# Attention beside dense products: remainders on GpSimd, rows of ones kept, a norm square with priority

## The chip, the cores and the metric

The kernel runs on one core of a Trainium2 chip. A core has a matrix engine (TensorE, PE in the profile), a vector engine (VectorE, DVE), a scalar engine (ScalarE, ACT), GpSimd (POOL) and SyncE (SP, which issues most transfers). Each engine runs its own instructions strictly in order, and they wait for one another by semaphores. SBUF is the working memory of 128 partitions, PSUM holds the eight banks that TensorE writes. The metric is device time in microseconds (us), as a median over runs.

## The reference

The program is a decoder trunk of two layers on 512 tokens of width 1024, in float32. Each layer adds half a SwiGLU feed-forward network (FFN), then a mixer, then half of another FFN:

```
x = x + 0.5 * swiglu(rms_norm(x), ffn1_w_in, ffn1_w_out)
h = rms_norm(x) @ w_mix_in
y = concat[ short_conv(c_x, c_b, c_c), hgrn2(q, f, i, g), fox(q, k, v, f) ]
x = x + y @ w_mix_out
x = x + 0.5 * swiglu(rms_norm(x), ffn2_w_in, ffn2_w_out)
```

Only the mixer is touched by the change. Its three parts are:

- a gated causal convolution of width 3 over 256 channels;
- HGRN2, a linear recurrence with 4 heads of 64, whose output o of each head is normalised, o * rsqrt(mean(o * o) + eps), then scaled and gated;
- FoX attention with 8 heads of 64: logits q.k + c_t - c_s with c the running sum of log forget gates, a causal softmax, and the product with the values.

## The kernel before

**Exact products.** TensorE multiplies in a rounded format (fp32r), so each operand is split in two: a rounded part hi and the remainder lo = x - hi. A product is three matmuls (`mm3`, lines 322, 330 and 331): hi by hi, hi by the other's lo, lo by the other's hi. For weights the split is made while they stream: `granule` (line 286) loads two blocks of rows into one of two staging buffers `st` (line 294, on SyncE's queue), and `parted` (line 303) rounds them by ScalarE (line 311) and subtracts on VectorE (line 312) into one of three buffers `hl`. Both are issued under `high_priority`, so that they run ahead of the products that use them. A staging buffer is loaded again when its subtraction is done; an `hl` buffer is written again when its products are done.

**The mixer.** `mix` first projects features, then runs HGRN2 with the projections of attention's q, k and v (`fox_qkv`) beside it, and then attention with the remaining dense products beside it. `fox_attend` is a generator over 16 items (4 heads of one half, 4 blocks of 128 queries each); `beside` draws one dense granule per item. The first half of the heads has `conv` beside it: the features of the convolution, three streams of four granules, 256 columns wide. The second half has `most` beside it: four column groups of the output projection, over five of its eight row blocks, so three granules each (the third is of one row block, half as wide). After both, the last three row blocks of the output projection follow by themselves.

**Attention.** For each head, `fox_prep` makes four operands QA, QB, KA and KB: two transposed halves of q and k with their remainders, and in rows 64 and 65 of KB the negated running sums of log forget gates (a transfer, line 1556), against rows 64 and 65 of QB, which hold ones (a memset on GpSimd, line 1557). Two more transfers, lines 1565 and 1566, copy across partitions. Scores are two matmuls (lines 1586 and 1587) into a bank with the tag "sc"; VectorE subtracts the row maximum from it (line 1591), ScalarE exponentiates, and P is scaled by the reciprocal of its sum (lines 1595 to 1599). Then TensorE transposes P into a bank with the tag "pt" (line 1651), ScalarE rounds (1653) and VectorE subtracts (1654), and the products with the values follow (1609). PSUM has three banks "mm", two "sc", two "pt" and one "po".

**The norm of HGRN2.** At the end of `hgrn`, TensorE puts the means of o * o into two banks "pt" (line 1463). Then come ln and exp on ScalarE for a first inverse root r, the square of r (line 1471, an `act`, which the profile shows as line 274), and on VectorE, for each of the two halves, (mean + eps) * r * r (line 1473), which is the last reading of a bank. Lines 1476 to 1485 finish and split the result. These run while the first items of attention go by.

**What sets the order.** A planner places the instructions of each engine before the run: it takes the work in program order as its rank, `high_priority` raises the rank of what is issued under it, and of the instructions that are ready in its own reckoning the best rank goes first. On the chip the order is then fixed.

Of the kernel before, what the change touches and what calls it, by code (L numbers as in the profile page):

```python
# [8 lines left out]
F32 = mybir.dt.float32  # L9
F32R = mybir.dt.float32r  # L10
# [13 lines left out]
P = 128  # L24
# [133 lines left out]
class Trunk:  # L158
# [124 lines left out]
        self.chain[engine] = i.ins.name  # L283


    def granule(self, parts, kk, ahead=True, skew=0, keep=False, queued=False, first=False):
        nc = self.nc
        c = sum(ap.shape[1] for ap in parts)
        st = self.wp.tile([P, 1024], F32, tag="st", name=self.n("st"), bufs=2)
        s3 = st[:, : kk * c].rearrange("p (k c) -> p k c", k=kk)  # L290
        at = 0
        for ap in parts:
            w = ap.shape[1]
            d = nc.sync.dma_start(s3[:, :, at : at + w], ap.rearrange("(k p) c -> p k c", p=P))
            if queued:
                self.follow("s", d)
            at += w
        with self.tc.high_priority() if ahead and not keep else ExitStack():
            hi, lo = self.parted(st[:, : kk * c], 1 if ahead else kk, skew, keep or first)
        h3, l3 = (a.rearrange("p (k c) -> p k c", k=kk) for a in (hi, lo))  # L300
        return [(h3[:, i, :], l3[:, i, :]) for i in range(kk)]

    def parted(self, src, pieces=1, skew=0, keep=False):
        nc = self.nc
        n = src.shape[1]
        hl = self.wp.tile([P, 2 * 1024 + 64], F32R, tag="hl", name=self.n("hl"), bufs=3)
        hh, ll = (hl[:, a + skew : a + skew + n] for a in (0, 1024))
        w = n // pieces
        for c in range(0, n, w):
            hi, lo = hh[:, c : c + w], ll[:, c : c + w]  # L310
            a = nc.scalar.copy(hi, src[:, c : c + w])  # L311
            b = nc.vector.tensor_sub(lo, src[:, c : c + w], hi)  # L312
            if pieces > 1 or keep:
                self.follow("a", a)
                self.follow("v", b)
        return hh, ll
# [19 lines left out]
        for _ in self.stream_steps(*args, **kw):  # L336
            pass

    def stream_steps(self, jobs, parts_of, act, nk, mid=None, pre=None, given=None, queued=False, ending=None):
        k = 0  # L340
        while k < nk:
            kk = min(2, nk - k)
            if callable(mid) and k == nk - 2:
                mid()
            if pre is not None:
                pre(k)
            end = k + kk == nk
            if end and ending is not None:
                jobs = ending
            skew = SKEW_MOVING if jobs[0][2] is not None and jobs[-1][0].shape[-1] < T else 0  # L350
            keep = given is not None and given(k)
            rows = self.granule(
                parts_of(k, kk), kk, pre is None, skew, keep, queued, queued and k == 0
            )
            if keep:
                yield
            order = (
                [(job, j) for job in jobs for j in range(kk)]
                if end
                else [(job, j) for j in range(kk) for job in jobs]  # L360
            )
            for n, ((acc, cols, toks, *more), j) in enumerate(order):
                if pre is not None and n == len(order) // 2:
                    pre(k, True)
                if isinstance(mid, tuple) and (k, len(order) // 2) == (mid[0], n):
                    mid[1]()
                ah, al = act(k + j)
                hi, lo = rows[j]
                first, last = k + j == 0 and not more, end and j == kk - 1
                if toks is None:  # L370
                    self.mm3(acc, hi[:, cols], lo[:, cols], ah, al, first, last)
                else:
                    self.mm3(acc, ah[:, toks], al[:, toks], hi[:, cols], lo[:, cols], first, last)
            k += kk
            yield
# [647 lines left out]
    def mix(self, l, w, w_out, conv_w, out_gain, q_gain, k_gain, f_bias, next_gain):  # L1023
# [3 lines left out]
        with tc.tile_pool(name=self.n("mix"), bufs=1) as mp:  # L1027
# [23 lines left out]
            def cols(*spans):  # L1051
                return lambda k, kk: [w[k * P : (k + kk) * P, a : a + n] for a, n in spans]

            def features_steps(spans, banks, mid=None):
                bs = [self.bank(t) for t in banks]
                yield from self.stream_steps(
                    [(b, c, None) for b, c in zip(bs, FM2)], cols(*spans), self.xact, KD, mid
                )
                return bs

# [77 lines left out]
            for part, n in enumerate(hgrn):  # L1138
                if n is None:
                    break  # L1140
                if n == 0:
                    left.close()
                    ap1 = left.enter_context(
                        tc.tile_pool(name=self.n("at"), bufs=1, reuse_waits="tile")
                    )
                    for tag in ("PH", "PL"):
                        ap1.tile([P, 4, 2, P], F32R, tag=tag, name=self.n(tag), bufs=2)
                    ops = {h: self.fox_prep(ap1, h, half[0][0], qkg, "sc") for h in range(2)}
                if part < 2:
                    next(decay, None)  # L1150
                for _ in range(n):
                    next(dense, None)
# [18 lines left out]
            def conv():  # L1171
                for i in range(2):
                    bx, bc = yield from features_steps(
                        [(C_X + i * P, P), (C_C + i * P, P)], ("mm", "mm")
                    )
                    if i == 0:
                        inv2 = ap2.tile([P, T], F32, tag="t", name=self.n("iv2"), bufs=self.tb)
                        nc.scalar.activation(inv2, inv, AF.Square)
                    self.conv_in(ap2, i, bx, bc, inv2, cw)
                bb = yield from features_steps([(C_B, 256)], ("mm", "mm"))  # L1180
                for i in range(2):
                    self.conv_out(ap2, i, bb[i])

# [19 lines left out]
            def act(k0):  # L1203
                return lambda k: (self.yh[order[k0 + k]], self.yl[order[k0 + k]])
# [4 lines left out]
            def most():  # L1209
                for dg in range(4):  # L1210
                    banks = [self.bank("mm") for _ in range(2)]
                    yield from self.stream_steps(
                        [(bk, c, None) for bk, c in zip(banks, FM2)],
                        rows(0, 256 * dg, 256), act(0), 5,
                    )
                    for i in range(2):
                        add(2 * dg + i, banks[i])
# [47 lines left out]
    def hgrn(self, l, hp, hb, z, q, v, sg, og):  # L1265
# [202 lines left out]
        for x in range(2):  # L1468
            self.act(span(r, x), mb[x], AF.Ln, bias=self.epsc)
        self.act(r, r, AF.Exp, scale=-0.5)  # L1470
        self.act(t, r, AF.Square)
        for x in range(2):
            nc.vector.scalar_tensor_tensor(
                out=span(t, x), in0=mb[x], scalar=EPS, in1=span(t, x), op0=ALU.add, op1=ALU.mult
            )
        nc.vector.tensor_scalar(t, t, scalar1=-0.5, scalar2=1.5, op0=ALU.mult, op1=ALU.add)
        nc.vector.tensor_mul(r, r, t)
        nc.vector.tensor_mul(o, o, r)
# [73 lines left out]
    def fox_prep(self, pool, h, qk, g, tag="pt"):  # L1552
        nc = self.nc
        tl = lambda p, tag: pool.tile([p, T], F32R, tag=tag, name=self.n(tag), bufs=2)
        QA, QB, KA, KB = tl(P, "QA"), tl(66, "QB"), tl(P, "KA"), tl(66, "KB")
        nc.sync.dma_start(KB[64:66, :].bitcast(F32), self.negc[h : h + 1, :, :].bitcast(F32))
        nc.gpsimd.memset(QB[64:66, :].bitcast(F32), 1.0)
        b = self.bank(tag)
        for i in range(4):
            nc.tensor.transpose(  # L1560
                b[:, i * P : (i + 1) * P], qk[:, i, h % 4].rearrange("p w d -> p (w d)"), self.ident
            )
        nc.scalar.activation(QA[:64, :], b[:64, :], AF.Copy, scale=g[:64, :])
        nc.scalar.activation(KA[64:, :], b[64:, :], AF.Copy, scale=g[64:, :])
        nc.sync.dma_start(QB[:64, :].bitcast(F32), QA[:64, :].bitcast(F32))
        nc.sync.dma_start(KA[:64, :].bitcast(F32), KA[64:, :].bitcast(F32))
        nc.vector.scalar_tensor_tensor(
            out=QA[64:, :], in0=b[:64, :], scalar=g[:64, :], in1=QA[:64, :],
            op0=ALU.mult, op1=ALU.subtract,
        )  # L1570
        nc.vector.scalar_tensor_tensor(
            out=KB[:64, :], in0=b[64:, :], scalar=g[64:, :], in1=KA[64:, :],
            op0=ALU.mult, op1=ALU.subtract,
        )
        return QA, QB, KA, KB
# [297 lines left out]
```

## Time and profile before

| what | value |
|---|---|
| median of 3 runs | 1807.59 us (1806.88 to 1808.02) |
| the profiled execution, its own time | 1808.44 us |
| its span, first to last instruction | 1806.7 us |
| granted TensorE clock | 1.00 |
| TensorE busy | 1795.8 us (99%) |
| VectorE busy | 1453.4 us (80%) |
| ScalarE busy | 1000.7 us (55%) |
| GpSimd busy | 170.4 us (9%) |
| HBM read | 223.98 MB |

The profile is one execution. A row of instructions names the line, the engine, the operation, what is written and read, the shape, the count, the busy time and the mean duration in ns, and then how long the engine stood idle before them and which work ended that idle time. A row of waits names who waited for whom, the sum in us, how often, and the longest. Matmuls are pipelined: the next begins before the last has ended, so the time between two starts tells more than a duration.

### The profile page before, as it was taken

What the parts mean: (1) busy time and instruction counts of PE and PEld (TensorE: products, weight loads), DVE (VectorE), ACT (ScalarE), POOL (GpSimd) and SP (SyncE); (2) the same over time, 40 slices, a digit from 0 to 9 for tenths busy, and PEclk for the clock granted to TensorE, in tenths of its full rate; (3) what the DMA queues carried; (4) which work ended last, traced back from release to release, by engine and by line L of the source; (5) the groups of instructions that cost most, each with busy time, mean ns of one, the idle gap of its engine ahead of it and who ended that gap; (6) DMA issues with size and microseconds to landing.
All of it is one profiled execution on the core that took longest, in us unless ns stands there. A gap on an engine that the chain in (4) does not pass through costs nothing.

```text
span 1806.7 us, 34748 instructions
## 1 busy us (share of the span) xinstructions
PE 1795.8 (99%) x14267; PEld 1681.3 (93%) x14267; DVE 1453.4 (80%) x2036; ACT 1000.7 (55%) x1437; POOL 170.4 (9%) x172
## 2 busy tenths in 40 slices
PE   9999999999999999999999999999999999999999
PEld 7899999899888899999889999998998888999997
DVE  8889787776887898879679887876868878888893
ACT  5455554464786465556446555555547855555551
POOL 0011120100000001112001111201000000020210
PEclk9999999999999999999999999999999999999999
DMA  7668783233323767868265787823333247687762
GB/s 203 182 142 186 178 178 98 72 79 83 88 74 111 218 140 161 198 160 169 82 205 133 165 189 191 169 66 81 78 89 89 71 138 188 164 159 192 159 134 94
DMA packets 243486, 250.94 MB, mean 139 GB/s; under 512 B 18520, under 2 KB 228192, under 8 KB 243328
## 3 DMA queue, kind: packets, MB, share of 16 engines
q1 hardware_dynamic: 189424, 182.38, 33.8%
q0 software_dynamic: 53600, 66.09, 23.2%
q8 instruction: 112, 1.84, 0.4%
q14 instruction: 46, 0.38, 0.1%
q10 hardware_dynamic: 304, 0.27, 0.0%
HBM read 223.98 MB, written 2.10 MB: 125 GB/s over the span
## 4 chain that ended last, share of the span: by engine, by line
PE 92%; DVE 3%; ACT 3%; issue 1%; DMA 1%; SPq 0%; ACTq 0%; DVEq 0%
PE mm L322 13%; PE mm L330 13%; PE mm L331 13%; PE sc L330 6%; PE sc L331 6%; PE sc L322 6%; PE pt L322 6%; PE pt L330 6%; PE pt L331 6%; PE po L330 4%; PE po L322 4%; PE po L331 4%; ACT hl L311 1%; PE po L1609 1%; PE pt L1651 1%
## 5 line engine op out<-in xcount | busy, mean ns | idle before, releaser
L803 ACT CAST hl<-w 128x1024 fp32r<-128x1024 f32 x322 | 336.7, 1050 | 313.7 <-PE mm L331 82.4
L805 DVE TENSOR_TENSOR hl<-w,hl 128x1024 fp32r<-128x1024 f32 x322 | 392.2, 1221 | 80.7 <-ACT hl L803 80.7
L312 DVE TENSOR_TENSOR hl<-st,hl 128x512 fp32r<-128x512 f32 (+3 forms) x192 | 162.3, 845 | 106.3 <-ACT hl L311 105.5
L311 ACT CAST hl<-st 128x512 fp32r<-128x512 f32 (+3 forms) x192 | 142.6, 743 | 169.9 <-PE po L331 64.6
L322 PE MATMUL mm<-xc,hl 128*128 128x256 f32 (+1 forms) x733 | 201.2, 276 | 0.0
L330 PE MATMUL mm<-xc,hl 128*128 128x256 f32 x728 | 201.2, 276 | 0.0
L331 PE MATMUL mm<-xc,hl 128*128 128x256 f32 x728 | 201.0, 276 | 0.0
L322 PE MATMUL sc<-xc,hl 128*128 128x256 f32 (+1 forms) x532 | 146.0, 276 | 0.0
L330 PE MATMUL sc<-xc,hl 128*128 128x256 f32 x528 | 146.0, 276 | 0.0
L331 PE MATMUL sc<-xc,hl 128*128 128x256 f32 x528 | 145.9, 276 | 0.0
L322 PEld LDWEIGHTS mm<-xc,hl 128*128 128x128 f32 x733 | 137.4, 188 | 0.2
L330 PEld LDWEIGHTS mm<-xc,hl 128*128 128x128 f32 x728 | 136.7, 188 | 0.0
L331 PEld LDWEIGHTS mm<-xc,hl 128*128 128x128 f32 x728 | 136.7, 188 | 0.0
L322 PE MATMUL pt<-xc,hl 128*128 128x256 f32 (+1 forms) x482 | 132.6, 276 | 0.0
L330 PE MATMUL pt<-xc,hl 128*128 128x256 f32 x480 | 132.6, 276 | 0.0
L331 PE MATMUL pt<-xc,hl 128*128 128x256 f32 x480 | 132.5, 276 | 0.0
L322 PE MATMUL mm<-x,hl 128*128 128x512 f32 x272 | 107.4, 395 | 0.0
L331 PE MATMUL mm<-x,hl 128*128 128x512 f32 x272 | 106.4, 391 | 0.0
L330 PE MATMUL mm<-x,hl 128*128 128x512 f32 x272 | 106.1, 390 | 0.0
L322 PEld LDWEIGHTS sc<-xc,hl 128*128 128x128 f32 x532 | 99.7, 188 | 0.2
L331 PEld LDWEIGHTS sc<-xc,hl 128*128 128x128 f32 x528 | 99.1, 188 | 0.1
L330 PEld LDWEIGHTS sc<-xc,hl 128*128 128x128 f32 x528 | 99.2, 188 | 0.0
(513 smaller groups left out, 5594.1 us busy)
## 6 DMA issues: line engine op xcount, KB each, us to landing
w<-in_ffn_w_in_dram SPq DMA_DIRECT2D x140, 512.0 KB
w<-in_ffn_w_out_dram SPq DMA_DIRECT2D x64, 512.0 KB
w<-in_ffn_w_out_dram POOLq DMA_DIRECT2D x56, 512.0 KB, 8.3
st<-in_w_mix_in_dram SPq DMA_DIRECT2D x88, 256.0 KB
st<-in_ffn_w_in_dram SPq DMA_DIRECT2D x70, 256.0 KB
w<-in_ffn_w_in_dram POOLq DMA_DIRECT2D x35, 512.0 KB, 8.5
w<-S POOLq DMA_DIRECT2D x35, 512.0 KB, 4.7
st<-in_ffn_w_out_dram SPq DMA_DIRECT2D x24, 512.0 KB
```

The lines of the kernel that those rows point to most:

```text
L311: a = nc.scalar.copy(hi, src[:, c : c + w])
L312: b = nc.vector.tensor_sub(lo, src[:, c : c + w], hi)
L322: i = nc.tensor.matmul(acc[:, c], ah, bh[:, c], start=first and c.start == 0, stop=False, skip_group_check=True,)
L330: nc.tensor.matmul(acc, a, b, start=False, stop=False, skip_group_check=True)
L331: i = nc.tensor.matmul(acc, c, d, start=False, stop=last, skip_group_check=True)
L803: A(nc.scalar.copy(hi, src))
L805: return lambda: V(nc.vector.tensor_sub(lo, src, hi))
L1609: nc.tensor.matmul(self.ob[:, t0 + u * P : t0 + 2 * P], V[:, j, h % 4].rearrange("p a d -> p (a d)"), part[:, j, u:, :].rearrange("p i t - ...
L1651: nc.tensor.transpose(tb[:, j * P : (j + 1) * P], p[:, j * P : (j + 1) * P], self.ident)
```

## The change

It has four parts, all in the mixer, and so each occurs once per layer.

1. `granule`, `parted`, `stream_steps` and `features_steps` take an argument `lows`, the engine that subtracts. `conv` and `most` pass GpSimd; every other stream keeps VectorE. So 12 granules of `conv` and 12 of `most` have their remainders from GpSimd, in each layer. Their rounding stays on ScalarE, and their priority stays.
2. The tiles QB are no longer allocated for each head. Two are made once per layer, in the pool of attention, and used in turn.
3. Their rows of ones are written there, two memsets in each layer in place of eight.
4. In `hgrn`, the square of r and the two operations of line 1473 are issued under `high_priority`.

```
     def granule(self, parts, kk, ..., first=False, lows=None):
...
-            hi, lo = self.parted(st[:, : kk * c], 1 if ahead else kk, skew, keep or first)
+            hi, lo = self.parted(
+                st[:, : kk * c], 1 if ahead else kk, skew, keep or first, lows or nc.vector
+            )
...
-    def parted(self, src, pieces=1, skew=0, keep=False):
+    def parted(self, src, pieces=1, skew=0, keep=False, lows=None):
...
             a = nc.scalar.copy(hi, src[:, c : c + w])
-            b = nc.vector.tensor_sub(lo, src[:, c : c + w], hi)
+            b = (lows or nc.vector).tensor_tensor(lo, src[:, c : c + w], hi, op=ALU.subtract)
...
                         ap1.tile([P, 4, 2, P], F32R, tag=tag, name=self.n(tag), bufs=2)
+                    self.qb = pair(ap1, "QB", F32R)
+                    for t in self.qb:
+                        nc.gpsimd.memset(t[64:66, :].bitcast(F32), 1.0)
                     ops = {h: self.fox_prep(ap1, h, half[0][0], qkg, "sc") for h in range(2)}
...
                     bx, bc = yield from features_steps(
-                        [(C_X + i * P, P), (C_C + i * P, P)], ("mm", "mm")
+                        [(C_X + i * P, P), (C_C + i * P, P)], ("mm", "mm"), lows=nc.gpsimd
                     )
...
-                bb = yield from features_steps([(C_B, 256)], ("mm", "mm"))
+                bb = yield from features_steps([(C_B, 256)], ("mm", "mm"), lows=nc.gpsimd)
...
-                        rows(0, 256 * dg, 256), act(0), 5,
+                        rows(0, 256 * dg, 256), act(0), 5, lows=nc.gpsimd,
...
-        self.act(t, r, AF.Square)
-        for x in range(2):
-            nc.vector.scalar_tensor_tensor(
-                out=span(t, x), in0=mb[x], scalar=EPS, in1=span(t, x), op0=ALU.add, op1=ALU.mult
-            )
+        with self.tc.high_priority():
+            self.act(t, r, AF.Square)
+            for x in range(2):
+                nc.vector.scalar_tensor_tensor(
+                    out=span(t, x), in0=mb[x], scalar=EPS, in1=span(t, x),
+                    op0=ALU.add, op1=ALU.mult,
+                )
...
-        QA, QB, KA, KB = tl(P, "QA"), tl(66, "QB"), tl(P, "KA"), tl(66, "KB")
+        QA, KA, KB = tl(P, "QA"), tl(P, "KA"), tl(66, "KB")
+        QB = self.qb[h % 2][:66, :]
         nc.sync.dma_start(KB[64:66, :].bitcast(F32), self.negc[h : h + 1, :, :].bitcast(F32))
-        nc.gpsimd.memset(QB[64:66, :].bitcast(F32), 1.0)
```

More of the change, by code (lines that the diff above doesn't have):

```diff
@@ L283, in follow, with granule @@
         self.chain[engine] = i.ins.name
-    def granule(self, parts, kk, ahead=True, skew=0, keep=False, queued=False, first=False):
+    def granule(self, parts, kk, ahead=True, skew=0, keep=False, queued=False, first=False, lows=None):
         nc = self.nc
@@ L337, in stream, with stream_steps @@
             pass
-    def stream_steps(self, jobs, parts_of, act, nk, mid=None, pre=None, given=None, queued=False, ending=None):
+    def stream_steps(self, jobs, parts_of, act, nk, mid=None, pre=None, given=None, queued=False, ending=None, lows=None):
         k = 0
@@ L352, in stream_steps @@
             rows = self.granule(
-                parts_of(k, kk), kk, pre is None, skew, keep, queued, queued and k == 0
+                parts_of(k, kk), kk, pre is None, skew, keep, queued, queued and k == 0, lows
             )
@@ L1052, in cols, with features_steps @@
                 return lambda k, kk: [w[k * P : (k + kk) * P, a : a + n] for a, n in spans]
-            def features_steps(spans, banks, mid=None):
+            def features_steps(spans, banks, mid=None, lows=None):
                 bs = [self.bank(t) for t in banks]
                 yield from self.stream_steps(
-                    [(b, c, None) for b, c in zip(bs, FM2)], cols(*spans), self.xact, KD, mid
+                    [(b, c, None) for b, c in zip(bs, FM2)], cols(*spans), self.xact, KD, mid,
+                    lows=lows,
                 )
```

## The prediction

> **What bounds the kernel now.** I read the page's engine shares, then TensorE's own waits, then busy time by stretches of the two attention stages, then the order of time where TensorE stands longest, and last what GpSimd does there.
>
> ```profile
> span 1806.7 us, 34748 instructions
> PE 1795.8 (99%) x14267; PEld 1681.3 (93%) x14267; DVE 1453.4 (80%) x2036; ACT 1000.7 (55%) x1437; POOL 170.4 (9%) x172
> ```
>
> TensorE is busy for 1795.8 of 1806.7 us; all that other engines can give back is the 10.9 us in which it stands, and a little that its pipelined ends hide. What it waits for:
>
> ```profile
> PE pt L1651 <- DVE T L1473: 2.6, 2, 1.5
> PE mm L1765 <- DVE z L1752: 1.2, 1, 1.2
> PE po L1609 <- ACT PH L1653: 0.8, 2, 0.4
> PE sc L1586 <- DVE nm L1591: 0.7, 2, 0.4
> PE pt L1651 <- DVE KB L1571: 0.4, 2, 0.2
> PE mm L322 <- DVE zf L1125: 0.4, 1, 0.4
> PE sc L1586 <- DVE fo L1623: 0.2, 1, 0.2
> PE po L1609 <- DVE PL L1654: 0.2, 1, 0.2
> ```
>
> Line 1765 is the opening of the kernel and line 1125 lies ahead of attention. All else, 4.9 us, lies in the two attention stages, one per layer. The reader should see that the largest, 2.6 us, is two waits, one per layer, of a transpose for the HGRN2 norm, and that VectorE ends nearly all the others. Here are the two stages, and the first layer's worst 20 us (columns: stretch, its length, busy time and instructions of TensorE, its weight loads, VectorE, ScalarE, GpSimd, then the granted clock, DMA share and GB/s):
>
> ```profile
> 460.00:568.00 108.00, 105.15 (x585) 87.79 (x585) 90.09 (x222) 82.11 (x186) 3.13 (x6) 1.00 0.33 90
> 1352.00:1461.00 109.00, 106.39 (x595) 88.72 (x594) 91.07 (x223) 82.72 (x187) 3.12 (x6) 1.00 0.34 90
> 470.00:480.00 10.00, 8.47 (x47) 7.09 (x46) 9.55 (x24) 7.23 (x19) 0.52 (x1) 1.00 0.34 81
> 480.00:490.00 10.00, 9.82 (x51) 7.86 (x51) 9.87 (x19) 8.61 (x17) 0.53 (x1) 1.00 0.33 80
> ```
>
> VectorE is busy 83% of a stage, but 97% from 470 to 490 us, where the norm's last operations and the first granules meet; GpSimd is all but idle. The clock is 1.00 throughout, so time is not lost there.
>
> **The norm square with priority.** The row of TensorE's 2.6 us, in order of time (start, duration, engine, line):
>
> ```profile
> 466.77 1.04 ACT L274 ACTIVATE T<-T 128x1024 f32<-128x1024 f32 x1
> 467.72 0.79 ACT L1597 ACTIVATE P<-P,rs 128x128 f32<-128x128 f32 x2
> 470.25 1.05 ACT L274 ACTIVATE T<-T 128x1024 f32<-128x1024 f32 x1
> 471.33 0.69 DVE L1473 SCALAR_TENSOR_TENSOR T<-pt,T 128x512 f32<-128x512 f32 x1 [0.18 <-ACT T L274]
> 474.13 0.68 DVE L1473 SCALAR_TENSOR_TENSOR T<-pt,T 128x512 f32<-128x512 f32 x1
> ...
> 470.21 0.22 PE L1586 MATMUL sc<-KA,QA 128*128 128x128 f32 x1
> 470.27 0.28 PE L1587 MATMUL sc<-KB,QB 66*128 66x128 f32 x1
> 472.08 0.33 PE L1651 MATMUL pt<-ident,P 128*128 128x128 f32 x1 [1.53 <-DVE T L1473]
> ...
> 1362.87 0.28 PE L1587 MATMUL sc<-KB,QB 66*128 66x128 f32 x1
> 1364.24 0.33 PE L1651 MATMUL pt<-ident,P 128*128 128x128 f32 x1 [1.10 <-DVE T L1473]
> ```
>
> The norm's means lie in both "pt" banks, and attention's transposes need such a bank. Line 1473 reads a bank for the last time, but waits for the square (470.25), which stands behind two scalings, an exponential, a rounding and two value copies, though its input was done at 467.81. With priority, the square can follow the exponential at once or after one short scaling: 467.85 to 468.6, ending by 469.7; line 1473 then runs at about 469 to 470.4 (0.69 + 0.68 us), before TensorE asks at 470.5. What is pushed back by 1.05 us is the scaling of P at 467.72, which then ends by about 469.6, still ahead. The wait goes in both layers. Its real price is taken from starts: 470.27 to 472.08 is 1.81 us, where a product of this size is followed after 0.06 us (470.21 to 470.27), so 1.75; in the second layer 1.37 - 0.06 = 1.31. Gain: 3.06 us; bounds 0 (the order stays) and 3.06. Next late is line 1591's reduction of the fourth score block on VectorE, which frees the next score bank; I charge 0.2 us over both layers for it. Bounds for that: 0, and 0.7, the row of all waits for line 1591. The two products with priority cost VectorE nothing; they only go ahead of value copies that nothing on TensorE awaits soon.
>
> **The remainders by GpSimd.** Each layer has 12 granules of the convolution's features and 12 of the first five rows of the output projection, four of these half as wide. Their subtraction (line 312) leaves VectorE. The rows of it, and of what it meets:
>
> ```profile
> L312 DVE TENSOR_TENSOR hl<-st,hl 128x512 fp32r<-128x512 f32 (+2 forms) x27 | 18.6, 689 | 6.4 <-ACT hl L311 6.1
> L1477 DVE TENSOR_TENSOR T<-T,T 128x1024 f32<-128x1024 f32 x1 | 1.2, 1212 | 0.0
> L1478 DVE TENSOR_TENSOR T<-T,T 128x1024 f32<-128x1024 f32 x1 | 1.2, 1227 | 0.0
> L1479 DVE SCALAR_TENSOR_TENSOR T<-T,og,sg 128x1024 f32<-128x1024 f32 x1 | 1.3, 1280 | 0.0
> L1485 DVE TENSOR_TENSOR hy<-T,hy 128x1024 fp32r<-128x1024 f32 x1 | 1.2, 1226 | 0.0
> L1242 DVE TENSOR_TENSOR cu<-cu,cy 128x512 f32<-128x512 f32 x2 | 1.4, 684 | 0.0
> ```
>
> Some 24 of the 27 go: 24 x 0.689 = 16.5 us less the four narrow ones' 4 x 0.3, so about 15.4 us a layer, and most of the 6.1 us in which VectorE stood before them for ScalarE's rounding. VectorE falls from 90 to about 75 us of 108. This is off the path by itself. On the path it takes from the waits that VectorE ends: 0.7 + 0.4 + 0.2 + 0.2 = 1.5 us in seven waits, and each hides about 0.2 us more under a modelled end (above, 1.75 against 1.53, and 1.31 against 1.10), so 2.9 us. I take two thirds, 1.9, since a score reduction late for its own input stays late; bounds 0 and 2.9, or 4.1 if ScalarE, which also stands behind VectorE, gives up its two waits of 0.8 + 0.4.
>
> What does it cost on GpSimd? No row shows a two-input operation there. Nearest:
>
> ```profile
> L1557 POOL MEMSET QB<- 2x512 f32 x16 | 8.3, 524 | 279.0 <-DVE ft L424 132.1 <-PE pt L1651 71.9 <-PE sc L1587 34.1
> L1037 POOL COPY zm<-maskb 128x128 bf16<-128x128 bf16 x2 | 0.6, 297 | 0.0
> L1376 POOL MEMSET lf<- 128x128 f32 x2 | 0.4, 208 | 80.1 <-ACT T L274 80.1
> ```
>
> Writing 512 elements a partition takes 0.52 us; reading 128 beside writing adds 0.297 - 0.208 = 0.09 us, so two reads of 512 add 0.71: 1.23 us as an estimate. Bounds: 0.69 (VectorE's row) and 1.6 (three passes of 0.52). So a remainder is done some 0.55 us later than before. The Trainium skill (GPSIMD Engine Reference, 3.1 Elementwise) gives 2.6 cycles an element at 1.2 GHz for two inputs, an estimate of 1.1 us for 512; by it the sum would be the same. The cover for the delay is long:
>
> ```profile
> ACT hl L311 <- PE mm L331: 6.6, 9, 1.4
> DVE hl L312 <- ACT hl L311: 6.1, 6, 2.2
> 472.33 0.68 DVE L312 TENSOR_TENSOR hl<-st,hl 128x512 fp32r<-128x512 f32 x1
> 479.75 0.48 PE L322 MATMUL mm<-x,hl 128*128 128x512 f32 x1
> ```
>
> Rounding waits for TensorE to free one of three hl buffers, so preparation runs two granules ahead: the convolution's fourth remainder ends at 473.01 and its products start at 479.75. Cost 0; without this cover it would be 48 x 0.55 = 26 us. GpSimd itself has 24 x 1.23 = 30 us of work in 108. Behind a remainder waits, on SyncE, the load into the staging buffer, and behind that the copies of QB, KA and KB for the next head, later by up to 0.55 us; these are used a head later. Only the first two heads of the second half are prepared shortly before use, so I charge 0.2 us over both layers; bounds 0 and 2.2 (two heads, two layers, 0.55 each). On GpSimd's queue nothing urgent stands behind a remainder: the next FFN's accumulating loads come after the last one.
>
> **Rows of ones once per layer.** Six memsets a layer of 0.52 us go. No wait of TensorE names them, so the gain is 0. Left in place they would hold the remainders: GpSimd stood 279 us before them. The copy into QB still waits for the same products, as KB's copy does.
>
> **Sum.** -3.06 + 0.2 - 1.9 + 0.2 = -4.6 us. The profiled execution took 1808.44 us, 0.85 above the median of 1807.59: 1803.84 there, 1803.0 as a median.
>
> **Rivals.** (1) VectorE's relief is hidden by ScalarE's and the program's order, and only the norm's waits go: -3.06 + 0.4 = -2.7, 1804.9. For it: ScalarE is 76% busy and in order. (2) More goes: -3.06 - 4.1 = -7.2, 1800.4. For it: VectorE is 97% busy just where TensorE stands. (3) Slower: a GpSimd operation that reads and a VectorE operation with two inputs in SBUF exclude each other. From 470 to 490 us lie five of these (1477, 1478, 1479, 1485, 1242), and five remainders leave, 3.4 us. If each of the five waits for a whole remainder at its upper bound, 5 x 1.6 - 3.4 = 4.6 us a layer is added where VectorE has no slack, 9.2 in all, less 3.06: 1813.7. It decides from a wait of about 1.0 us for each. Against it: a remainder fills only a third of the time between granules, and the products of attention read a PSUM bank and so one input from SBUF. The Trainium skill (SBUF — State Buffer, Who interferes with whom) states this exclusion and that the loser blocks for the whole instruction; no run here shows it yet. (4) The order is planned before the run, and the square stays where it is: -1.9 + 0.4 = -1.5, 1806.1. For it: the exponential ahead of it keeps its old rank.
>
> **How the numbers follow.** My forecast has 0.45 (its own range is 1801.3 to 1804.8), rival 1 0.20, rival 2 0.12, rival 3 0.13, rival 4 0.10. Leaving out rival 3's far end and a little below rival 2 gives 1799.8 to 1809.5. A measurement here tells 0.2%, 3.6 us, from no change: faster means below 1804.0. That takes four fifths of the forecast, rival 2 and a quarter of rival 1: 0.36 + 0.12 + 0.05 = 0.53. Slower takes rival 3, 0.13, and 0.01 for anything else; the rest, 0.33, is the same.
>
> **What would show it.** Right: the wait of line 1651 for line 1473 is gone in both layers; the square starts within 0.5 us of its exponential's end; remainders on GpSimd last 1.1 to 1.4 us; VectorE falls to about 75 us in the stage; TensorE's idle there falls by half or more. Wrong: remainders above 2 us, the VectorE rows quoted above growing longer, or TensorE waiting for hl's remainder at line 331.

## The result: slower by 0.37%, and the profile after

| kernel | median | ratio to before, 95% interval |
|---|---|---|
| before | 1807.47 us | |
| changed | 1814.11 us | 1.0037 [1.0026, 1.0048] |

The changed kernel is 6.7 us slower; 4.6 us faster was forecast. The page of the changed kernel, its span and engine shares, then TensorE's longest waits, then the two attention stages (stretch, length, TensorE, its weight loads, VectorE, ScalarE, GpSimd, granted clock, DMA share, GB/s). New line numbers: 1659 and 1480 were 1651 and 1473, 1594 was 1586, 1617 was 1609, 1662 was 1654, 1579 was 1571.

```profile
span 1814.0 us, 34742 instructions
PE 1799.4 (99%) x14267; PEld 1681.6 (93%) x14267; DVE 1438.0 (79%) x1988; ACT 1001.7 (55%) x1437; POOL 222.5 (12%) x208
```

```profile
PE pt L1659 <- DVE T L1480: 2.1, 2, 1.1
PE pt L1659 <- DVE KB L1579: 2.0, 6, 0.5
PE sc L1594 <- DMA KA<-KA: 1.5, 4, 0.7
PE po L1617 <- DVE PL L1662: 1.4, 2, 0.7
```

```profile
460.00:568.00 108.00, 103.88 (x573) 85.27 (x572) 81.35 (x195) 82.22 (x185) 29.19 (x24) 1.00 0.32 86
1352.00:1461.00 109.00, 105.09 (x594) 87.36 (x594) 82.54 (x199) 83.40 (x185) 29.72 (x25) 1.00 0.31 84
```

The reader is to see three things. The clock is 1.00, so nothing is lost there. TensorE stands 4.12 us of the first stage instead of 2.85. And the norm's wait, which was to vanish, is still 2.1 us, while three waits that were 0.4, nothing and 0.2 have grown to 2.0, 1.5 and 1.4. VectorE is relieved, but to 81 us and not to 75.

VectorE's own groups say most of why 81. In the first layer's attention stage of the changed kernel (last columns: busy us, mean ns, idle before), and below it the one row of before that the prediction didn't show:

```profile
L1254 DVE SCALAR_TENSOR_TENSOR cy<-cu,cw,cy 128x510 f32<-128x510 f32 x2 | 2.5, 1268 | 0.0
L1248 DVE TENSOR_TENSOR cu<-cu,cy 128x512 f32<-128x512 f32 x2 | 2.5, 1235 | 0.1
L1485 DVE TENSOR_TENSOR T<-T,T 128x1024 f32<-128x1024 f32 x1 | 2.2, 2197 | 0.0
L1487 DVE SCALAR_TENSOR_TENSOR T<-T,og,sg 128x1024 f32<-128x1024 f32 x1 | 2.2, 2172 | 0.0
```

```profile
L1248 DVE SCALAR_TENSOR_TENSOR cy<-cu,cw,cy 128x510 f32<-128x510 f32 x2 | 1.5, 746 | 0.0
```

Lines 1242, 1477 and 1479 of before took 684, 1212 and 1280 ns; as 1248, 1485 and 1487 they take 1235, 2197 and 2172. All four groups read two inputs from SBUF. A mean of two hides that only one of each pair is long: 1.78 beside 0.69 us at line 1248, 1.78 beside 0.75 at line 1254. With one of line 1251, by 0.15 us, five operations of the stage are longer, by 4.2 us together. One of them in order of time in the changed kernel, with a remainder on GpSimd beside it:

```profile
507.18 1.29 POOL L314 TENSOR_TENSOR hl<-st,hl 128x512 fp32r<-128x512 f32 x1 [5.20 <-ACT hl L313]
507.23 1.78 DVE L1254 SCALAR_TENSOR_TENSOR cy<-cu,cw,cy 128x510 f32<-128x510 f32 x1
508.94 0.28 DVE L1599 CUSTOM_DVE_ANT_0 P<-sc,zm 128x128 f32<-128x128 f32 x1
509.15 0.41 DVE L1662 TENSOR_TENSOR PL<-pt,PH 128x256 fp32r<-128x256 f32 x1
509.62 0.39 PE L1617 MATMUL po<-PL,V 128*128 128x256 f32 x1 [0.71 <-DVE PL L1662]
```

GpSimd starts 0.05 us earlier, VectorE's operation takes 1.78 instead of 0.75 us, the subtraction behind it is late, and TensorE stands 0.71 us. That is the exclusion of rival 3. The Trainium skill (SBUF — State Buffer, Who interferes with whom) states it for a VectorE instruction with two SBUF inputs and a GpSimd instruction that reads; these rows agree in the main, as the second one ends 0.54 us after the remainder, where it takes 0.75 us alone.

### The profile page after: what moved, and what is told of

It reads as the page before. It is cut to its first block, busy times and chain, and to the rows that moved or that the text cites. A ratio compares the mean times of both kernels' runs of the same rounds, so it can differ in the third digit from the quotient of the medians.

```text
span 1814.0 us, 34742 instructions
## 1 busy us (share of the span) xinstructions
PE 1799.4 (99%) x14267; PEld 1681.6 (93%) x14267; DVE 1438.0 (79%) x1988; ACT 1001.7 (55%) x1437; POOL 222.5 (12%) x208
## 4 chain that ended last, share of the span: by engine, by line
PE 93%; DVE 3%; ACT 2%; DMA 1%; issue 1%; SPq 0%; ACTq 0%; DVEq 0%
PE mm L324 13%; PE mm L333 13%; PE mm L332 13%; PE sc L333 6%; PE sc L332 6%; PE sc L324 6%; PE pt L324 6%; PE pt L332 6%; PE pt L333 6%; PE po L324 4%; PE po L333 4%; PE po L332 4%; PE pt L1659 1%; PE po L1617 1%; DMA KA<-KA 1%
## 5 line engine op out<-in xcount | busy, mean ns | idle before, releaser
L314 DVE TENSOR_TENSOR hl<-st,hl 128x512 fp32r<-128x512 f32 (+2 forms) x144 | 131.2, 911 | 94.9 <-ACT hl L313 94.4
L822 POOL DMA_DIRECT2D w<-S x35 | 31.1, 887 | 598.6 <-DVE hl L807 520.0
L324 PEld LDWEIGHTS sc<-xc,hl 128*128 128x128 f32 x532 | 99.7, 188 | 0.2
L333 PEld LDWEIGHTS sc<-xc,hl 128*128 128x128 f32 x528 | 99.1, 188 | 0.0
```

What stands on the lines that cost most here:

```text
L314: b = (lows or nc.vector).tensor_tensor(lo, src[:, c : c + w], hi, op=ALU.subtract)
L324: i = nc.tensor.matmul(acc[:, c], ah, bh[:, c], start=first and c.start == 0, stop=False, skip_group_check=True,)
L333: i = nc.tensor.matmul(acc, c, d, start=False, stop=last, skip_group_check=True)
L822: G(nc.gpsimd.dma_start(raw[u, 1], sums[u], accum_op=ALU.add))
```

## The experiments

All 14 runs are held against the kernel before on the same chip. A single ratio is uncertain by about 0.09%, 1.6 us. So the table gives beside it what TensorE stands in both attention stages in the profiled execution. It is read from starts: whatever two successive starts lie apart beyond the usual pace (0.23 us for 512 columns), where it is over 0.12 us. The three parts are the norm's (440 to 475 us and 1335 to 1370), the convolution's (475 to 520, 1370 to 1415) and the output projection's (520 to 580, 1415 to 1475), in us over both layers. Line numbers differ by a few lines from kernel to kernel, so the rows are best told by what they write and read.

| kernel | norm | conv | rows | sum | ratio, 95% interval |
|---|---|---|---|---|---|
| before | 3.1 | 2.1 | 4.4 | 9.5 | |
| changed | 2.8 | 5.3 | 6.6 | 14.8 | 1.0037 [1.0026, 1.0048] |
| without the priority | 2.2 | 3.3 | 6.2 | 11.7 | 1.0021 [1.0012, 1.0029] |
| without GpSimd | 1.0 | 3.0 | 4.1 | 8.1 | 0.9997 [0.9988, 1.0006] |
| GpSimd, old order | 2.9 | 3.8 | 3.9 | 10.6 | 1.0010 [1.0001, 1.0019] |
| VectorE, new order | 2.7 | 4.3 | 7.4 | 14.4 | 1.0026 [1.0015, 1.0037] |
| new order, first part | 2.3 | 4.5 | 4.2 | 11.0 | 1.0012 [1.0003, 1.0021] |
| new order, second part | 2.7 | 2.3 | 6.9 | 11.9 | 1.0016 [1.0007, 1.0025] |
| norm alone | 2.6 | 2.6 | 4.2 | 9.3 | 1.0003 [0.9994, 1.0012] |
| norm and reduction | 2.3 | 2.1 | 4.6 | 9.0 | 0.9995 [0.9986, 1.0004] |
| GpSimd reads beside | 3.6 | 6.7 | 5.6 | 15.9 | 1.0035 [1.0023, 1.0048] |
| no remainders | 2.7 | 1.2 | 3.2 | 7.1 | 0.9988 [0.9979, 0.9997] |
| none, GpSimd reads | 2.7 | 2.8 | 3.4 | 9.0 | 0.9999 [0.9990, 1.0007] |
| GpSimd, conv, old order | 2.6 | 4.5 | 4.6 | 11.7 | 1.0016 [1.0007, 1.0025] |
| GpSimd, rows, old order | 2.4 | 2.3 | 3.2 | 7.9 | 0.9992 [0.9983, 1.0001] |
| rows and norm | 2.1 | 1.8 | 4.1 | 8.0 | 0.9991 [0.9982, 0.9999] |

**Parts undone, and order against work.** The first two runs take one part of the change out:

```diff
-        with self.tc.high_priority():
-            self.act(t, r, AF.Square)
...
+        self.act(t, r, AF.Square)
...
```

> The changed kernel without the priority of the norm square (remainders on GpSimd and kept rows of ones stay). Three theories. L: GpSimd itself costs (a GpSimd operation that reads and VectorE operations with two SBUF inputs hold each other up, and SyncE's loads wait longer). O: the planner's new order costs, not the engine. N: the priority of the norm square disturbs the order. L and O expect about 1814 here, N expects 1807 or less.

```diff
-                        [(C_X + i * P, P), (C_C + i * P, P)], ("mm", "mm"), lows=nc.gpsimd
+                        [(C_X + i * P, P), (C_C + i * P, P)], ("mm", "mm")
...
-                bb = yield from features_steps([(C_B, 256)], ("mm", "mm"), lows=nc.gpsimd)
+                bb = yield from features_steps([(C_B, 256)], ("mm", "mm"))
...
-                        rows(0, 256 * dg, 256), act(0), 5, lows=nc.gpsimd,
+                        rows(0, 256 * dg, 256), act(0), 5,
```

> The changed kernel with all remainders back on VectorE (kept rows of ones and priority stay). L expects the gain of the norm alone, 1804.5 to 1807. O has no number of its own: about as many TensorE instructions (16) are moved by it as a third of those of the full change (52), so at most a third of the loss, 1807 to 1809.5. N expects 1812 or more.

Either removal helps, but without the priority the kernel is still 1.0021. In the changed kernel, 52 instructions on TensorE, 56 on VectorE, 50 on ScalarE and 2 loads on SyncE stand at other places in their queues than before: the planner had ordered the stages anew. So the next two kernels hold the work and the order apart. Every instruction of the stages gets a dependency without a semaphore on the one that is to stand ahead of it, so that the queue has a given order (`ORDERS` lists the instructions of each engine in both stages):

```diff
+def pin(tc):
...
+    for row in ORDERS:
...
+            if before is not None:
+                tc.add_manual_dep(placed[name], before, NOSYNC, reason="given order")
+            before = name
...
         trunk_kernel(tc, *args, out)
+        pin(tc)
```

One has the remainders on GpSimd in the order of before, the other has them on VectorE in the changed kernel's order. Both keep the rows of ones once per layer.

> The changed kernel with the order of the kernel before given to TensorE, VectorE, ScalarE and SyncE; the remainders are on GpSimd. (With that order the priority is without effect.) L expects the loss to stay: 1811 or more. O expects it gone: 1804 to 1808, the time before less what VectorE's relief gives.

> The reverse: all remainders on VectorE, and the order of the changed kernel given to TensorE, ScalarE, SyncE and to VectorE's other instructions. L expects the loss gone: 1804 to 1808. O expects it to stay: 1812 or more.

1.0010 and 1.0026 add up to 1.0036, the change's 1.0037 within the uncertainty. Some 4.7 of the 6.7 us, with an interval of 2.7 to 6.7, are the new order, with VectorE doing what it always did. The kernel before was not run with its own order given, but the kernel below in which the norm's operations alone move has them too, and comes out at 1.0003 [0.9994, 1.0012], so the dependencies by themselves cost nothing that shows.

**Where the order costs.** The moves fall into short closed stretches, so they can be put back in halves. Each of the next two is the kernel before with a given order, as above, in one part of the stages.

> The kernel before, remainders on VectorE, but with the changed kernel's order on TensorE, VectorE and ScalarE in the first part of each attention stage (the norm and the convolution, to some 40 us after its start), and the old order behind that. The whole new order cost 4.7 us. If the priority of the norm's square is what does the harm, most of it is here: 1811 to 1812. If the part that GpSimd's remainders alone bring (the output projection's first rows) does it, 1807.6 to 1809: the stretch from 475 to 520 us then holds some 1.2 us more standing of TensorE a layer by starts, and the norm's own gives 0.4 back.

> The other half: the old order up to the convolution's end, and the changed kernel's order behind it, where the products of the second granules of the output projection stand 17 to 23 places earlier or later among attention's and one load stands ahead of two copies. If the second part costs: 1810 to 1811.5, with TensorE standing some 1.5 us more a layer from 515 to 580 us (0.97 against 0.17 us before a transpose of P at 515, and 0.75 and 0.47 at 528 to 530). If the first part does: 1807.6 to 1808.5. The two halves together should give 4.7 us over the kernel before.

Both halves cost, about 2.2 and 2.9 us, each uncertain by 1.6. The 0.97 us at 515 us that I had placed in the second part appeared in the first, since ScalarE's and VectorE's moves of the first part reach that far. How a move costs is plainest in the second: VectorE and ScalarE in order of time, in the kernel with the new order there, and then in the kernel before.

```profile
524.03 0.69 DVE L312 TENSOR_TENSOR hl<-st,hl 128x512 fp32r<-128x512 f32 x1
524.75 0.76 DVE L1571 SCALAR_TENSOR_TENSOR KB<-pt,qkg,KA 64x512 fp32r<-64x512 f32 x1
525.54 0.22 DVE L1595 RECIPROCAL rs<-rs 128x1 f32<-128x1 f32 x2
...
525.74 0.80 ACT L1597 ACTIVATE P<-P,rs 128x128 f32<-128x128 f32 x2 [0.94 <-DVE rs L1595]
...
526.19 0.33 PE L1651 MATMUL pt<-ident,P 128*128 128x128 f32 x1 [0.57 <-ACT P L1597]
```

```profile
526.53 0.69 DVE L312 TENSOR_TENSOR hl<-st,hl 128x512 fp32r<-128x512 f32 x1
527.13 0.16 DVE L1595 RECIPROCAL rs<-rs 128x1 f32<-128x1 f32 x1
...
527.67 0.16 DVE L1595 RECIPROCAL rs<-rs 128x1 f32<-128x1 f32 x1
527.86 0.75 DVE L1571 SCALAR_TENSOR_TENSOR KB<-pt,qkg,KA 64x512 fp32r<-64x512 f32 x1
```

KB of a later head was moved four places ahead, past a reduction and the reciprocals of the two blocks that TensorE is about to transpose. ScalarE stands 0.94 us for the reciprocal, TensorE 0.57 us by the profile and 0.74 by starts. A 0.76 us operation put ahead of one of 0.16 us does that, with no engine busier than before.

**The norm by itself.** The kernel before with a given order in which only three operations move in each layer: ScalarE's square, five places ahead, and the two of line 1473.

> The kernel before, with its order kept on every engine, but the square of the norm moved on ScalarE right behind the first scaling of P, and the two operations of line 1473 moved on VectorE ahead of the third reciprocal, in both layers: the prediction's first term by itself. If that term was right (1.75 and 1.31 us of standing, read from starts, go, and line 1591 gives 0.2 back): 1804.8, a ratio of 0.9984. If a wait that is taken away comes back a few microseconds later, as with the priority alone, where a third of it was left: 1806.5 to 1807.6. In both, VectorE's waits in the second half of the stage stay as before.

The norm's wait is gone and the time is not: 1.0003 [0.9994, 1.0012]. Its longest waits of TensorE, the same stretch in order of time, and last the third reciprocal and the fourth reduction in the kernel before:

```profile
PE sc L1586 <- DVE nm L1591: 1.7, 4, 0.5
PE po L1609 <- ACT PH L1653: 1.5, 4, 0.4
```

```profile
467.50 1.29 DVE L1473 SCALAR_TENSOR_TENSOR T<-pt,T 128x512 f32<-128x512 f32 x2 [2.03 <-ACT T L274]
468.70 0.15 DVE L1595 RECIPROCAL rs<-rs 128x1 f32<-128x1 f32 x1
...
472.36 0.68 DVE L1591 CUSTOM_DVE_ANT_0 P<-sc,zm 128x512 f32<-128x512 f32 x1
...
473.10 0.39 PE L1586 MATMUL sc<-KA,QA 128*128 128x256 f32 x1 [0.49 <-DVE nm L1591]
474.27 0.38 PE L1609 MATMUL po<-PH,V 128*128 128x256 f32 x1 [0.33 <-ACT PH L1653]
```

```profile
469.14 0.16 DVE L1595 RECIPROCAL rs<-rs 128x1 f32<-128x1 f32 x1 [2.08 <-ACT P L274]
473.32 0.68 DVE L1591 CUSTOM_DVE_ANT_0 P<-sc,zm 128x512 f32<-128x512 f32 x1
```

TensorE now comes to the fourth score block's reduction sooner, but the reduction isn't done sooner. The two kernels are compared from the start of the third block's reduction, 464.45 here and 466.05 before. The norm's square now stands ahead of the third block's exponential on ScalarE, and its two operations ahead of that block's reciprocal on VectorE. So the reciprocal starts after 4.25 us instead of 3.09, and the fourth reduction after 7.91 instead of 7.27. By starts TensorE stands 0.74 us there and then 0.54 for PH, instead of 1.75 at the norm; in the second layer 0.73 and 0.54 instead of 1.31. The next run moves that reduction too, and the exponential behind it:

> The norm alone moved TensorE's wait from line 1473 to line 1591 and to PH, 0.74 + 0.54 us in place of 1.75 in the first layer. Here the fourth score block's reduction (line 1591, with its reading) is moved as well, ahead of the four value copies on VectorE, and the exponential behind it ahead of the third value copy on ScalarE, in both layers. If the value copies are all that makes it late, those 1.28 and 1.27 us go too: 1805.2, 0.9987. If the next operation is late in turn: 1806.5 to 1807.6.

0.9995 [0.9986, 1.0004], so still not told from no change. TensorE's longest wait in this kernel:

```profile
PE pt L1651 <- DVE rs L1595: 2.0, 2, 1.2
```

The wait moved on once more, to the reciprocal. In these two kernels attention's chain from one score block to its transposes sets the pace at this place, and the norm's operations lie in the same queues. It is no fixed bound: in the order that the planner chose without GpSimd, TensorE stands only 1.0 us in the norm's part, but 0.9 us more than before at the convolution, and the time, 0.9997, can't be told from before either.

**VectorE's relief and GpSimd's hold.** Three kernels in the order of before. They are made from the changed kernel without the priority, so they keep the rows of ones once per layer. The first adds GpSimd's reading to the full work of VectorE:

```diff
-            b = (lows or nc.vector).tensor_tensor(lo, src[:, c : c + w], hi, op=ALU.subtract)
+            b = nc.vector.tensor_sub(lo, src[:, c : c + w], hi)
+            if lows:
+                h = hi[96:128, :]
+                lows.tensor_tensor(self.qb[0][96:128, :w], h, h, op=ALU.subtract)
```

> The kernel before in its own order, VectorE still doing the remainders, and 48 operations on GpSimd beside them, at the moments and of the length of the changed kernel's remainders: they read the rounded weights twice and write to rows that nothing reads, so that nothing waits for them. This is GpSimd's use of the memory without the late remainders. If two-input operations of VectorE are held by it (theory L): lines 1477, 1479, 1242 and 1248 take up to a microsecond more where they meet, and 1808.3 to 1809.0, most of the 1.4 us that the remainders on GpSimd cost in the old order. If those 1.4 us come from remainders that are done later, and from the loads and copies behind them: 1807.6, as before. If only GpSimd's partitions count, the 32 that are read here may hold VectorE less.

The second takes the remainders away, and the third adds to it the reading of the first:

```diff
-            b = (lows or nc.vector).tensor_tensor(lo, src[:, c : c + w], hi, op=ALU.subtract)
+            b = a if lows else nc.vector.tensor_sub(lo, src[:, c : c + w], hi)
...
-        return hh, ll
+        return hh, hh if lows else ll
```

> The kernel before in its own order, with the 48 remainders left out: the low halves of those weights are not computed and TensorE reads the rounded halves in their place, so the number of products is the same and the output is another. VectorE is relieved of 15.4 us a layer, as the prediction wanted, and nothing is put on GpSimd: the prediction's third term by itself. If that term was right (1.9 us, between 0 and 4.1): 1805.7, or down to 1803.5. If TensorE's waits were not a matter of VectorE's load (the view after the first runs, since VectorE's relief showed in no time): 1807.6.

> As the one above, remainders left out, but with the 48 operations of GpSimd that read and that nothing waits for. Against the one above it is GpSimd's hold on VectorE without the remainders' own collisions and without late remainders; against the remainders on GpSimd in the old order (1809.0) it lacks only that they are done later. If the hold makes the loss (VectorE's rows grew by some 4 us a layer): 2 to 4 us above the one without remainders, and 1808.5 to 1809. If lateness does: at most 0.5 us above the one without remainders.

Leaving the remainders out gives 0.9988 [0.9979, 0.9997], 2.2 us: the relief is real, and my view after the first runs, that VectorE's load didn't matter, fell. GpSimd's reading gives it back to 0.9999 (1807.28 against 1805.60 us), though nothing waits for its results. Beside a fully loaded VectorE the same reading costs 1.0035, as much as the whole change. There it also meets VectorE's own remainders, which begin at the same rounding. Their group in that kernel, in the first layer's stage (689 ns in the kernel before):

```profile
L314 DVE TENSOR_TENSOR hl<-st,hl 128x512 fp32r<-128x512 f32 x21 | 18.2, 869 | 4.4 <-ACT hl L313 4.3
```

Real remainders on GpSimd in the old order are at 1.0010, 2 us above the third of these. Two kernels tell whether a longer hold or the later remainders make that difference. They have the remainders on GpSimd, in the old order, for the convolution alone:

```diff
-                        rows(0, 256 * dg, 256), act(0), 5, lows=nc.gpsimd,
+                        rows(0, 256 * dg, 256), act(0), 5,
```

> The kernel before in its own order, remainders on GpSimd only for the convolution's 24 granules. Here lie the two-input operations of VectorE that were held (lines 1248, 1251, 1254, 1487). If the hold is what takes VectorE's relief back: 1808.5 to 1809.5, these lines 0.3 to 1.0 us longer, and TensorE standing 0.6 us or more in front of a product of PL at 508 us.

or for the output projection's rows alone:

```diff
-                        [(C_X + i * P, P), (C_C + i * P, P)], ("mm", "mm"), lows=nc.gpsimd
+                        [(C_X + i * P, P), (C_C + i * P, P)], ("mm", "mm")
...
-                bb = yield from features_steps([(C_B, 256)], ("mm", "mm"), lows=nc.gpsimd)
+                bb = yield from features_steps([(C_B, 256)], ("mm", "mm"))
```

> The same with GpSimd only for the output projection's 24 granules, where VectorE has hardly an operation that it could hold. If the hold is what takes the relief back: 1806.3 to 1807.0, half of the 1.9 us that leaving the remainders out gave. If remainders that are done 0.55 us later, with the loads and copies behind them, are what does it: 1807.6 to 1808.5, with TensorE waiting for the copies of KA, as in the changed kernel.

It is the hold. The convolution's remainders on GpSimd are at 1.0016 [1.0007, 1.0025], the rows' at 0.9992 [0.9983, 1.0001], with 1.6 us less of TensorE standing. VectorE's groups in the first layer, with the convolution's remainders on GpSimd, and then with the rows' (line 1485 here was 1479 before):

```profile
L1248 DVE TENSOR_TENSOR cu<-cu,cy 128x512 f32<-128x512 f32 x2 | 2.5, 1238 | 0.1
L1254 DVE SCALAR_TENSOR_TENSOR cy<-cu,cw,cy 128x510 f32<-128x510 f32 x2 | 2.4, 1223 | 0.0
L1485 DVE SCALAR_TENSOR_TENSOR T<-T,og,sg 128x1024 f32<-128x1024 f32 x1 | 2.3, 2290 | 0.0
L1251 DVE SCALAR_TENSOR_TENSOR cy<-cu,cw,cy 128x511 f32<-128x511 f32 x2 | 2.0, 1008 | 0.7 <-ACT cy L1250 0.7
```

```profile
L1251 DVE SCALAR_TENSOR_TENSOR cy<-cu,cw,cy 128x511 f32<-128x511 f32 x2 | 1.5, 748 | 0.2 <-ACT cy L1250 0.2
L1254 DVE SCALAR_TENSOR_TENSOR cy<-cu,cw,cy 128x510 f32<-128x510 f32 x2 | 1.5, 744 | 0.0
L1248 DVE TENSOR_TENSOR cu<-cu,cy 128x512 f32<-128x512 f32 x2 | 1.4, 684 | 0.0
L1485 DVE SCALAR_TENSOR_TENSOR T<-T,og,sg 128x1024 f32<-128x1024 f32 x1 | 1.3, 1277 | 0.0
```

Each row of two is again a long operation and one of the old length. So four operations of the stage are longer in the first than in the second, by 1.10, 0.97, 0.51 and 1.01 us, 3.6 together. Each of the four began while a remainder ran on GpSimd, and the same four are longer in the second layer. With the rows' remainders on GpSimd none is. In neither kernel does TensorE wait for a remainder.

**What they point to.** GpSimd for the rows alone, in the order of before with the norm's operations, the fourth reduction and its exponential moved:

```diff
-                bb = yield from features_steps([(C_B, 256)], ("mm", "mm"), lows=nc.gpsimd)
+                bb = yield from features_steps([(C_B, 256)], ("mm", "mm"))
...
         trunk_kernel(tc, *args, out)
+        pin(tc)
```

> The kernel that the runs so far point to: the old order with the norm's operations and the fourth reduction moved, and GpSimd making the remainders of the output projection's granules alone. If both gains hold and add up (0.7 us from the one, 0.9 from the other): 1806.0, a ratio of 0.9991. If neither is real: 1807.6.

0.9991 [0.9982, 0.9999], 1805.72 us: faster than both kernels, by about as much as the rows alone. How much of it the norm's moves give was not resolved.

## Why the prediction was wrong

- **The cost that was in no term of the sum: the order.** The sum took the other engines' queues as they stood, with instructions removed or moved one by one, and rival 4 asked only whether the square would move. Moving work to another engine let the planner reorder every queue of the stage. That is worth 4.7 us, the largest part of the miss, and its price is not in any row of before. The miss is 11.3 us, from 4.6 faster to 6.7 slower. The order makes 4.7 of it, the norm's gain of 2.9 that did not come makes 2.9, and GpSimd's part, forecast at -1.7 and measured at 1.8 in the old order, makes 3.5; these add up to 11.1. Why the planner chose that order was not studied. No run has the convolution's remainders without the rows' in an order of the planner's own, so which of them moves what stays open.
- **Norm, -3.06 + 0.2.** The term was mis-sized by its second number. The wait for line 1473 can be removed as said, but alone it gives nothing: "next late is line 1591" was right, and of 3.06 us all but some 0.5 by starts came back there and at PH, where 0.2 was charged. The step that failed is that moving the square pushes back only a scaling, and that the two operations of line 1473 go ahead of nothing that TensorE awaits soon: with the norm alone moved they went ahead of the third block's exponential and reciprocal, and that reciprocal came 1.16 us later. In the changed kernel the wait was not even removed. The square began 0.4 us after its exponential, as the prediction asked, but the exponential itself was placed behind more of ScalarE's work and started at 469.06 instead of 466.77:

```profile
469.06 1.05 ACT L274 ACTIVATE T<-T 128x1024 f32<-128x1024 f32 x1
470.01 0.61 ACT L313 CAST hl<-st 128x512 fp32r<-128x512 f32 x1
470.52 1.06 ACT L274 ACTIVATE T<-T 128x1024 f32<-128x1024 f32 x1
...
470.70 1.27 POOL L314 TENSOR_TENSOR hl<-st,hl 128x512 fp32r<-128x512 f32 x1 [3.32 <-ACT hl L313]
...
471.61 1.29 DVE L1480 SCALAR_TENSOR_TENSOR T<-pt,T 128x512 f32<-128x512 f32 x2 [1.77 <-ACT T L274]
472.36 0.33 PE L1659 MATMUL pt<-ident,P 128*128 128x128 f32 x1 [1.00 <-DVE T L1480]
```

- **Relief, -1.9.** Right as a term: 2.2 us, with an interval of 0.5 to 3.8, without remainders. (Its rows count six waits that VectorE ends, not seven, so its own working gives 2.7 and 1.8 us instead of 2.9 and 1.9.) But in the convolution it is not to be had this way.
- **Remainders cost 0.** Right on lateness, as far as it shows: the rows' remainders are later too, and cost nothing that shows. A full-width one took 1.31 us where 1.23 was estimated. Wrong on the hold, which stood only as a rival with a chance of 0.13. GpSimd's group in the changed kernel:

```profile
L314 POOL TENSOR_TENSOR hl<-st,hl 128x512 fp32r<-128x512 f32 x40 | 52.5, 1312 | 133.4 <-ACT hl L313 133.4
```

- **Rival 3.** Its mechanism is shown, and its time, 1813.7, is nearly the one measured; but that is a coincidence. Its price asked for five operations a layer held for a whole remainder at 1.6 us. In the old order four were, for 0.5 to 1.1 us, and on the time that cost some 4 us less the relief: 1.8 us for all remainders. The rest of the 6.7 us is the order. Of the prediction's three signs of being wrong, the one that showed is that VectorE's quoted rows grew longer.
- **Copies of QB and KA, 0.2.** In the changed kernel TensorE waits 1.5 us for KA, within the bound of 2.2. It takes the order and GpSimd together: in each layer one load now stands ahead of these copies on SyncE, and it waits for a remainder on GpSimd. With GpSimd in the old order the wait is 0.5 us, and with VectorE in the new order it is 0.5 too. In order of time (SPq is SyncE's queue):

```profile
549.56 1.29 POOL L314 TENSOR_TENSOR hl<-st,hl 128x512 fp32r<-128x512 f32 x1 [3.07 <-ACT hl L313]
550.88 0.34 SPq L294 DMA_DIRECT2D st<-in_w_mix_out_dram  x1
551.27 0.48 SPq L1573 DMA_DIRECT2D QB<-QA  x1
...
551.86 0.53 SPq L1574 DMA_DIRECT2D KA<-KA  x1
...
554.42 0.30 PE L1594 MATMUL sc<-KA,QA 128*128 128x128 f32 x1 [0.72 <-DMA KA<-KA]
```

- **Rows of ones, 0.** This was not run alone, and stays open within the uncertainty of the runs that keep it.

## What to carry to other kernels

Where a planner fixes the order, an edit has two prices, that of the work and that of the new order, and the second can be the larger; hold the old order and measure the first by itself. Before work goes to GpSimd, list VectorE's operations with two SBUF inputs in the same stretch: where there are some on the path, leave it on VectorE, and where there are none, it may pay (here 0.9992, with an interval from 0.9983 to 1.0001). A wait that is removed is worth only what the next link of the same chain leaves of it, so follow the chain to the link that paces it.

## What was not expected of the hardware

GpSimd holds VectorE just as well with 32 partitions as with 128: reads of rows 96 to 127 alone made the operation below last 2064 ns (1280 before) in the first layer of the kernel in which GpSimd reads beside, with every remainder still on VectorE. It ended 1.07 us after GpSimd's operation; beside a remainder of 128 partitions, with the convolution's remainders on GpSimd, it ended 1.09 us after.

```profile
L1488 DVE SCALAR_TENSOR_TENSOR T<-T,og,sg 128x1024 f32<-128x1024 f32 x1 | 2.1, 2064 | 0.0
```

A VectorE operation that reads one of its inputs from a PSUM bank was not lengthened, as line 1480 of the changed kernel shows: its two operations, which start at 471.61 while the remainder of 470.70 runs until 471.97, take 1.29 us together, and took 0.69 and 0.68 before. That is an overlap of 0.36 us; the operations of line 1662 that ran wholly beside a remainder (128x256) took 0.42 us, as without one.

GpSimd is held in turn. With the convolution's remainders on GpSimd, one that started at 484.01 us, 0.57 us after VectorE's operation with two SBUF inputs (line 1491, 483.44 to 484.67), took 1.81 us instead of 1.30.
